# A hybrid retention, gating and gated-MLP layer on one core: every product walks its moving operand as two interleaved halves

## The chip, the cores and the metric

The kernel runs on one core of one Trainium2 chip. The metric is device time in microseconds. The kernel before takes 818.51 us, the median of 3 runs that lie between 818.5 and 818.79 us.

## The reference

One layer over 512 positions of width 1024. All weights and activations are float32.

```python
h = _rmsnorm(x, g_pre_mix)
proj = h @ w_in                       # 1024 x 7168, then split
q, k, v, g, u, sv, a_ret, a_sgu = jnp.split(proj, list(np.cumsum(IN_SPLITS)[:-1]), axis=-1)
y_ret = _retention_branch(q, k, v, g, ret_decay_logit, w_ret_o)
y_sgu = _sgu_branch(u, sv, sgu_ln_g, sgu_ln_b, w_spatial, b_spatial, w_sgu_o)
merged = jax.nn.sigmoid(a_ret) * y_ret + jax.nn.sigmoid(a_sgu) * y_sgu
x = x + _rmsnorm(merged @ w_out, g_post_mix)
h2 = _rmsnorm(x, g_pre_ffn)
x = x + _rmsnorm(_conv_gated_mlp(h2, w_up, conv_w, conv_b, w_down), g_post_ffn)
```

The retention branch has 4 heads, works in chunks of 128 positions and runs over the sequence in both directions. The gating branch mixes positions inside chunks of 128. The MLP has 2816 hidden channels in each of its two halves, with a depthwise convolution over three positions between the up projection and the gate.

## The kernel before

Nearly all of the time goes to products on TensorE. A product, in this text, is one matmul instruction: a stationary operand of 128 x 128, a moving operand of 128 partitions by 512 or 256 columns, and a result in one PSUM bank of 128 partitions by 512 float32. To compute in float32 at TensorE's fast rate for that type, each operand is split into a high and a low part of type float32r: ScalarE writes the high part, VectorE the difference (`split`, L100). A float32 product is then three instructions, high by high, high by low and low by high, that add up in the same bank (`mm3`, L230, and the same triple written out at L340, L543 to L545, L761, L924 to L926, L1169 and L1185).

The stages follow each other in this order:

- 17 warm-up products on constants in bfloat16 (L324).
- The projection to q and k (L342 for the first eighth of the contraction, then `mm3`), 512 columns wide but for the first 24 products, which are 256 wide.
- Six groups of 96 products for v, sv and g (`t_group`, L533), with the retention heads between them (`scores`, `states`, `values`; all 256 wide through `mm3`).
- The projections to u and to the two merge gates, and four fifths of the up projection, in a scheme that computes a 2 x 2 block product with seven smaller products in place of eight (class `Pair`, L746, products at L762, all 256 wide). Between them stand plain blocks of 24 products, 512 wide (`f_block`, L735).
- The output projection (class `Down`, L906, 512 wide), and the second norm.
- The rest of the up projection in `f_block`, and the down projection in the scheme of seven again (`products`, L1156, and `add_whole`, L1176, all 256 wide).

Two kinds of product are not split. Products of whole float32 (L438 and L840, 128 columns) take two instructions each in the profile. Transposes (L522, L668, L685, L992) go through TensorE too.

Weights arrive over one DMA queue in blocks of 128 x 1024 float32 (L149), a few blocks ahead of their use, and are split or summed on ScalarE, VectorE and GpSimd into slots of a rotating buffer. The start addresses of the slots are offset by 64 or 192 bytes for some forms (`AT_64`, `AT_192`, L140; pads at L65). The results in the banks are read by ScalarE and VectorE with plain access patterns over the columns. TensorE's instructions run in the order of the program, which a scheduler keeps to.

The first operand after the output in `nc.tensor.matmul` is the stationary one, the second the moving one. Before the change every moving operand and every output is a plain run of 128, 256 or 512 consecutive columns per partition.

Of the kernel before, what the change touches and what calls it, by code (L numbers as in the profile page):

```python
# [19 lines left out]
KD = D // P  # L20
# [27 lines left out]
def tile_block(ctx: ExitStack, tc, xT, x, wall, par, cs, wsp, bsp, gpost, gffn, out):  # L48
    nc = tc.nc
# [43 lines left out]

    def copy(o, i):
        return nc.scalar.activation(out=o, in_=i, func=AF.Copy)  # L95

    def as32(t):
        return t.bitcast(F32)
# [11 lines left out]
    i = 0  # L110
    while i < NW:
# [7 lines left out]
        elif i == UP0 + 2 * COUPLES[0][0]:  # L119
# [3 lines left out]
            i = UP0 + 2 * COUPLES[-1][1] + 2  # L123
# [104 lines left out]
        return w_ready.pop(i)  # L228

    def mm3(o, ah, al, bh, bl, start, stop, skip=False):  # L230
        nc.tensor.matmul(o, ah, bh, start=start, stop=False, skip_group_check=skip)  # L231
        nc.tensor.matmul(o, ah, bl, start=False, stop=False, skip_group_check=skip)  # L232
        nc.tensor.matmul(o, al, bh, start=False, stop=stop, skip_group_check=skip)  # L233


    part = const("part", [P, NPAR])
# [24 lines left out]
    xh, xl, xg = [], [], {}  # L261
# [15 lines left out]
    def x_low(k, t, f=slice(0, S)):  # L277
        return nc.vector.scalar_tensor_tensor(
            out=xl[k][:, f], in0=t[:, f], scalar=col(PRE + k), in1=as32(xh[k][:, f]), op0=ALU.mult, op1=ALU.subtract
        )  # L280
# [45 lines left out]
    for k in range(KD):  # L326
        if k != 1:
            xts.append(load_x(k))
        if k == 0:
            xts.append(load_x(1))  # L330
        xt = xts[k]
        if k > 1:
            x_low(k, xt)
        if k == 2:
            copy(hold[:, 0:16], as32(xl[1])[:, 0:16])
        wh, wl = w_get(1 if k < 4 else LOOK)
        if k == 0:
            for half in range(2):
                for f in (T0, T1) if half == 0 else (slice(0, S),):
                    for a, b in ((wh, xh), (wl, xh), (wh, xl)):  # L340
                        for m in range(4 * half, 4 * half + 4):
                            nc.tensor.matmul(  # L342
                                qk[m][:, f], a[:, m * P : (m + 1) * P], b[0][:, f],
                                start=a is wh and b is xh and f.start == 0, stop=False, skip_group_check=True,
                            )
            continue
        if k > 1 and (k - 2) % 4 < 2:
            x_scaled(k - 2, xts[k - 2])
        for m in range(8):
            c = slice(m * P, (m + 1) * P)  # L350
            mm3(qk[m], wh[:, c], wl[:, c], xh[k], xl[k], False, k == KD - 1, True)
# [75 lines left out]
    for m in range(8):  # L427
        t = blk(n="qkraw")
# [6 lines left out]

    rb = ps()
    for t in range(NT):
        nc.tensor.matmul(  # L438
            rb[:, t * P : (t + 1) * P],
            rstd[:, t : t + 1].to_broadcast([P, P]),  # L440
            ident,
            start=True,
            stop=True,
        )
# [86 lines left out]
    part_end = [None]  # L531

    def t_group():  # L533

        acc = [ps() for _ in range(NT)]
        for kp in range(4):
            wh, wl = w_get()
            for t in range(NT):
                c = slice(t * P, (t + 1) * P)
                for kk in range(2):  # L540
                    k = 2 * kp + kk
                    f = slice(kk * S, (kk + 1) * S)
                    nc.tensor.matmul(acc[t], xh[k][:, c], wh[:, f], start=k == 0, stop=False)  # L543
                    nc.tensor.matmul(acc[t], xh[k][:, c], wl[:, f], start=False, stop=False)  # L544
                    part_end[0] = nc.tensor.matmul(acc[t], xl[k][:, c], wh[:, f], start=False, stop=k == KD - 1)  # L545
            yield acc

    vh, vl = {}, {}
# [143 lines left out]
    def row_sums():  # L692

        rw = ps()
        for n, w in enumerate(wst_parts):
            i = nc.tensor.matmul(rw, ones, w, start=n == 0, stop=n == 1)
        copy(rws, rw)
        return i.ins


    for h in range(H):
# [3 lines left out]
        acc = next(gen)  # L705
# [8 lines left out]
    ones, one = blk(F32R, "ones", (P, P)), blk(n="one", shape=(P, P))  # L714
# [6 lines left out]
    for n, acc in enumerate(t_group()):  # L721
# [3 lines left out]
        if n < 2:  # L725
            for k in (n + 2, n + 6):
                t = tmp("xT")
# [18 lines left out]
    class Pair:  # L746
# [8 lines left out]
        def product(self, b, act, first, w=None):  # L755
            wh, wl = w or w_get()
            o = self.b[b][:, T0]
            for k in range(4):
                c = slice(k * P, (k + 1) * P)
                h_, l_ = act(k)  # L760
                for n, (w_, a_) in enumerate(((wh, h_), (wh, l_), (wl, h_))):  # L761
                    self.last = nc.tensor.matmul(  # L762
                        o, w_[:, c], a_, start=first and k == n == 0, stop=k == 3 and n == 2,
                        skip_group_check=True,
                    )
            return o
# [53 lines left out]
    for j in range(KD // 2):  # L820
        p = Pair(AF.Gelu_apprx_tanh, lambda: U_HOMES.pop()(), None, rbc)
# [9 lines left out]
    def mix(j):  # L831
        gs = slice((j // 2) * P, (j // 2 + 1) * P)
        add = tmp("add", (P, P))
        v.scalar_tensor_tensor(
            out=add, in0=rws[:, gs], scalar=col(LNB + j), in1=bst[:, gs],
            op0=ALU.mult, op1=ALU.add,
        )
        o = ps()
        for t in range(NT):
            nc.tensor.matmul(  # L840
                o[:, t * P : (t + 1) * P],
                svz[t, j // 4][:, (j % 4) * P : (j % 4 + 1) * P],
                wst[:, gs],
                start=True,
                stop=True,
            )
        m = tmp("mix")
        v.scalar_tensor_tensor(
            out=m.rearrange("p (t q) -> p t q", t=NT),
            in0=o.rearrange("p (t q) -> p t q", t=NT),  # L850
            scalar=col(LNG + j),
            in1=add[:, None, :].to_broadcast([P, NT, P]),
            op0=ALU.mult,
            op1=ALU.add,
        )
        v.tensor_mul(uT[j], m, uT[j])
        h_, l_ = blk(F32R, "yh"), blk(F32R, "yl")
        split(h_, l_, uT[j])
        yh.append(h_)
        yl.append(l_)  # L860
# [22 lines left out]
    for j in range(KD // 2):  # L883
        for o, t in gated_pair(ogh, ogl, late if j == 0 else None):
            b = (lo64("r", F32) if j == 0 else hi192("r", F32) if j < 3 else blk(n="r"))
# [20 lines left out]
    class Down:  # L906
# [13 lines left out]
        def mms(self, t, k, n, bh, bl):  # L920
            c = slice(t * P, (t + 1) * P)
            ah, al = self.a[0][k][:, c], self.a[1][k][:, c]
            o = self.acc[t][n]
            nc.tensor.matmul(o, ah, bh, start=k == 0, stop=False)  # L924
            nc.tensor.matmul(o, ah, bl, start=False, stop=False)
            nc.tensor.matmul(o, al, bh, start=False, stop=k == self.nk - 1)  # L926

        def finish(self, t, n):
            for i, (wh, wl) in enumerate(self.held):
# [100 lines left out]
    for t in range(NT):  # L1030
        acc = [dn_.finish(t, 0)]
# [97 lines left out]
    i = 0  # L1129
    while i < NF:  # L1130
        if i in couples:
            p = Pair(None, lambda: tmp("c"), (h2h, h2l, h2forms))
            p.part1()
            o = [f_block(h2h, h2l, KD)]
# [5 lines left out]
        else:  # L1140
            o = []
# [14 lines left out]
    def products(m, j, steps={}, look=LOOK, ahead=None):  # L1156

        for n, (unit, at, act) in enumerate(UNITS):
            if n in (0, 3):
                with tc.issue_after(ahead) if ahead else ExitStack():  # L1160
                    wh, wl = w_get(look)
            if j == 0:
                m[n] = ps()
            f = slice(at * 256, (at + 1) * 256)
            ah, al = dforms[j][act]
            for t in range(2):
                c = slice(t * P, (t + 1) * P)
                o = m[n][:, t * 256 : (t + 1) * 256]
                for i, (a_, w_) in enumerate(((ah, wh), (ah, wl), (al, wh))):  # L1169
                    nc.tensor.matmul(  # L1170
                        o, a_[:, c], w_[:, f], start=j == t == i == 0,
                        stop=j == DP - 1 and i == 2 and n not in (M2, M3, M4), skip_group_check=True,
                    )
            steps.get(n, lambda: None)()

    def add_whole(m, t, gs, ws, last=False):  # L1176

        c = slice(t * P, (t + 1) * P)
        for n, b in enumerate(((M2, M3), (M4, M8))[t // 2]):
            o = m[b][:, (t % 2) * 256 : (t % 2 + 1) * 256]  # L1180
            for g, (wh, wl) in zip(gs, ws):
                for k in range(2):
                    f = slice(k * S + n * 256, k * S + (n + 1) * 256)
                    ah, al = whole[2 * g + k]
                    for i, (a_, w_) in enumerate(((ah, wh), (ah, wl), (al, wh))):  # L1185
                        nc.tensor.matmul(  # L1186
                            o, a_[:, c], w_[:, f], start=b == M8 and t == 2 and g == k == i == 0,
                            stop=last and g == gs[-1] and k == 1 and i == 2, skip_group_check=True,
                        )
# [27 lines left out]
    for j in range(DP):  # L1217
# [5 lines left out]
        if j in (3, 5):  # L1223
            w = w_get()
# [240 lines left out]
```

## Time and profile before

| | |
|---|---|
| median of 3 runs | 818.51 us |
| span of the profiled execution | 817.4 us |
| its TensorE clock, mean granted | 0.997 |
| TensorE products | 5163 instructions, 809.1 us busy |
| TensorE weight loads | 5163, 730.4 us busy |
| VectorE | 1115, 659.9 us busy |
| ScalarE | 777, 441.3 us busy |
| GpSimd | 93, 86.0 us busy |
| DMA | 93.24 MB, 114 GB/s on average |

The profile is one execution of the program. Times in its rows count from the start of the span. PE is TensorE's products, PEld its weight loads, DVE is VectorE, ACT is ScalarE, POOL is GpSimd. A row names the line of the kernel, the operation, the output and the inputs by the program's names, the size, and a count. Products overlap: the duration of one is longer than the distance to the next, so the rate of a stream of products is read from the distance between two starts.

### The profile page before, as it was taken

How to read it: one execution, taken by the hardware profiler on the slowest of the kernel's cores; microseconds unless marked ns; L12 is line 12 of the kernel's file. 1: busy time of each engine (PE TensorE's matmuls, PEld its weight loads, DVE VectorE, ACT ScalarE, POOL GpSimd, SP SyncE). 2: the span in 40 equal slices, each digit the busy share in tenths (PEclk: the TensorE clock that was granted, in tenths of full speed). 3: DMA queues.
4: the chain of work that ended last, by engine and by line, in shares of the span. 5: the costliest groups of instructions: out<-in, count | busy, mean ns of one | idle time of the engine just before them, and what ended most of it. 6: DMA issues, size and time to landing. Idle time of an engine off the chain costs nothing. (4 is left out here: it accounts for less than half of the span.)

```text
span 817.4 us, 13292 instructions
## 1 busy us (share of the span) xinstructions
PE 809.1 (99%) x5163; PEld 730.4 (89%) x5163; DVE 659.9 (81%) x1115; ACT 441.3 (54%) x777; POOL 86.0 (11%) x93
## 2 busy tenths in 40 slices
PE   9999999999999999999999999999999999999996
PEld 7888888888999999999988898899999898999996
DVE  7479897877898777767765659989999989987877
ACT  6546445536675444444445577556666666544441
POOL 0010000110001111132210210110111200000001
PEclk9999999999999999999999999999999999999998
DMA  8733222221333332233349111333333341233244
GB/s 287 259 117 103 78 79 77 77 79 65 103 103 105 104 103 90 91 103 103 107 165 335 53 51 66 104 103 104 104 103 103 103 156 52 77 130 110 97 155 155
DMA packets 29647, 93.24 MB, mean 114 GB/s; under 512 B 3536, under 2 KB 4432, under 8 KB 29584
## 3 DMA queue, kind: packets, MB, share of 16 engines
q1 hardware_dynamic: 27360, 86.76, 31.5%
q0 software_dynamic: 1360, 4.46, 1.6%
q10 hardware_dynamic: 864, 1.18, 0.4%
q8 instruction: 40, 0.66, 0.3%
q14 instruction: 23, 0.19, 0.1%
HBM read 88.19 MB, written 4.19 MB: 113 GB/s over the span
## 5 line engine op out<-in xcount | busy, mean ns | idle before, releaser
L102 DVE TENSOR_TENSOR wl<-raw,wh 128x1024 fp32r<-128x1024 f32 (+1 forms) x92 | 108.5, 1187 | 42.5 <-PE ps L762 20.0
L95 ACT ACTIVATE wf<-raw 128x512 fp32r<-128x512 f32 x140 | 85.0, 626 | 99.3 <-PE ps L232 34.0
L102 DVE TENSOR_TENSOR wf<-raw,wf 128x512 fp32r<-128x512 f32 x140 | 106.5, 773 | 25.3 <-ACT wf L95 24.5
L762 PE MATMUL ps<-sh,wf 128*128 128x256 f32 x640 | 118.8, 277 | 0.2 <-ACT c L95 0.2
L95 ACT ACTIVATE wh<-raw 128x1024 fp32r<-128x1024 f32 (+2 forms) x96 | 93.3, 983 | 39.2 <-PE ps L545 15.8
L762 PEld LDWEIGHTS ps<-sh,wf 128*128 128x128 f32 x640 | 100.9, 188 | 1.0 <-ACT c L95 0.4
L232 PE MATMUL ps<-h2l,wh 128*128 128x512 f32 (+1 forms) x256 | 92.5, 363 | 0.0
L231 PE MATMUL ps<-h2h,wh 128*128 128x512 f32 (+1 forms) x256 | 92.4, 364 | 0.0
L233 PE MATMUL ps<-h2h,wl 128*128 128x512 f32 (+1 forms) x256 | 92.3, 361 | 0.0
L762 PE MATMUL ps<-sl,wf 128*128 128x256 f32 x320 | 88.5, 277 | 0.0
L543 PE MATMUL ps<-wh,xh 128*128 128x512 f32 x192 | 75.0, 391 | 0.0
L544 PE MATMUL ps<-wl,xh 128*128 128x512 f32 x192 | 74.8, 390 | 0.0
L545 PE MATMUL ps<-wh,xl 128*128 128x512 f32 x192 | 74.7, 389 | 0.0
L762 PEld LDWEIGHTS ps<-sl,wf 128*128 128x128 f32 x320 | 60.1, 188 | 0.6
L1170 PE MATMUL ps<-dl,fh 128*128 128x256 f32 x216 | 59.8, 277 | 0.0
L1170 PE MATMUL ps<-dh,fh 128*128 128x256 f32 x216 | 59.7, 277 | 0.0
L1170 PE MATMUL ps<-dh,fl 128*128 128x256 f32 x216 | 59.7, 277 | 0.0
L233 PEld LDWEIGHTS ps<-h2h,wl 128*128 128x128 f32 x256 | 48.0, 188 | 7.7
L231 PEld LDWEIGHTS ps<-h2h,wh 128*128 128x128 f32 x256 | 47.8, 188 | 7.2 <-ACT h2h L994 0.3
L232 PEld LDWEIGHTS ps<-h2l,wh 128*128 128x128 f32 x256 | 48.1, 188 | 6.6
L762 PE MATMUL ps<-xh,wf 128*128 128x256 f32 x288 | 53.9, 278 | 0.0
L95 ACT ACTIVATE dh<-raw 128x768 fp32r<-128x768 f32 (+1 forms) x36 | 33.6, 949 | 34.4 <-DVE raw L204 18.9
(314 smaller groups left out, 2037.4 us busy)
## 6 DMA issues: line engine op xcount, KB each, us to landing
raw<-wall SPq DMA_DIRECT2D x144, 512.0 KB, 3.6
x<-x SPq DMA_DIRECT2D x24, 256.0 KB, 6.2
x<-x POOLq DMA_DIRECT2D x8, 256.0 KB, 2.4
xT<-xT SPq DMA_DIRECT2D x7, 256.0 KB, 4.7
xT<-xT POOLq DMA_DIRECT2D x4, 256.0 KB, 3.3
out<-zg SPq DMA_DIRECT2D x4, 256.0 KB, 2.0
raw<-wall SPq DMA_DIRECT2D x3, 256.0 KB, 4.7
out<-zs ACTq DMA_DIRECT2D x3, 256.0 KB, 2.4
```

The lines of the kernel that those rows point to most:

```text
L95: return nc.scalar.activation(out=o, in_=i, func=AF.Copy)
L102: nc.vector.tensor_sub(lo, src, as32(hi))
L231: nc.tensor.matmul(o, ah, bh, start=start, stop=False, skip_group_check=skip)
L232: nc.tensor.matmul(o, ah, bl, start=False, stop=False, skip_group_check=skip)
L233: nc.tensor.matmul(o, al, bh, start=False, stop=stop, skip_group_check=skip)
L543: nc.tensor.matmul(acc[t], xh[k][:, c], wh[:, f], start=k == 0, stop=False)
L544: nc.tensor.matmul(acc[t], xh[k][:, c], wl[:, f], start=False, stop=False)
L545: part_end[0] = nc.tensor.matmul(acc[t], xl[k][:, c], wh[:, f], start=False, stop=k == KD - 1)
L762: self.last = nc.tensor.matmul(o, w_[:, c], a_, start=first and k == n == 0, stop=k == 3 and n == 2, skip_group_check=True,)
L1170: nc.tensor.matmul(o, a_[:, c], w_[:, f], start=j == t == i == 0, stop=j == DP - 1 and i == 2 and n not in (M2, M3, M4), skip_group_check= ...
```

## The change

Two helpers are new. `two` regards the columns of an operand as two halves (n), each cut into pairs (c, with e the place in the pair), and orders them by pair first and half second: columns 0 and 1, then the first two of the second half, then columns 2 and 3, and so on. `mm` is a matmul whose output and moving operand are both regarded so. The stationary operand is not touched. As both are walked in the same order, each result lands in the column where it landed before, and the readers of the banks are unchanged.

```diff
     def copy(o, i):
         return nc.scalar.activation(out=o, in_=i, func=AF.Copy)
+
+    def two(t):
+        return t.rearrange("p (n c e) -> p c n e", n=2, e=2)
+
+    def mm(o, a, b, **kw):
+        return nc.tensor.matmul(two(o), a, two(b), **kw)
...
     def mm3(o, ah, al, bh, bl, start, stop, skip=False):
-        nc.tensor.matmul(o, ah, bh, start=start, stop=False, skip_group_check=skip)
-        nc.tensor.matmul(o, ah, bl, start=False, stop=False, skip_group_check=skip)
-        nc.tensor.matmul(o, al, bh, start=False, stop=stop, skip_group_check=skip)
+        mm(o, ah, bh, start=start, stop=False, skip_group_check=skip)
+        mm(o, ah, bl, start=False, stop=False, skip_group_check=skip)
+        mm(o, al, bh, start=False, stop=stop, skip_group_check=skip)
...
-                    nc.tensor.matmul(acc[t], xh[k][:, c], wh[:, f], start=k == 0, stop=False)
-                    nc.tensor.matmul(acc[t], xh[k][:, c], wl[:, f], start=False, stop=False)
-                    part_end[0] = nc.tensor.matmul(acc[t], xl[k][:, c], wh[:, f], start=False, stop=k == KD - 1)
+                    mm(acc[t], xh[k][:, c], wh[:, f], start=k == 0, stop=False)
+                    mm(acc[t], xh[k][:, c], wl[:, f], start=False, stop=False)
+                    part_end[0] = mm(acc[t], xl[k][:, c], wh[:, f], start=False, stop=k == KD - 1)
...
                 for n, (w_, a_) in enumerate(((wh, h_), (wh, l_), (wl, h_))):
-                    self.last = nc.tensor.matmul(
+                    self.last = mm(
                         o, w_[:, c], a_, start=first and k == n == 0, stop=k == 3 and n == 2,
                         skip_group_check=True,
                     )
```

In the same way `nc.tensor.matmul` becomes `mm` in the first eighth of the q and k projection (L342), at L438, L696 and L840, in `Down.mms` (L924 to L926), in `products` (L1170) and in `add_whole` (L1186). The warm-up products and the transposes stay as they were. Half of a 512-wide operand lies 1024 bytes behind the other half, half of a 256-wide one 512 bytes.

More of the change, by code (lines that the diff above doesn't have):

```diff
@@ L341, in tile_block @@
                         for m in range(4 * half, 4 * half + 4):
-                            nc.tensor.matmul(
+                            mm(
                                 qk[m][:, f], a[:, m * P : (m + 1) * P], b[0][:, f],
@@ L437, in tile_block @@
     for t in range(NT):
-        nc.tensor.matmul(
+        mm(
             rb[:, t * P : (t + 1) * P],
@@ L695, in row_sums @@
         for n, w in enumerate(wst_parts):
-            i = nc.tensor.matmul(rw, ones, w, start=n == 0, stop=n == 1)
+            i = mm(rw, ones, w, start=n == 0, stop=n == 1)
         copy(rws, rw)
@@ L839, in mix @@
         for t in range(NT):
-            nc.tensor.matmul(
+            mm(
                 o[:, t * P : (t + 1) * P],
@@ L923, in mms @@
             o = self.acc[t][n]
-            nc.tensor.matmul(o, ah, bh, start=k == 0, stop=False)
-            nc.tensor.matmul(o, ah, bl, start=False, stop=False)
-            nc.tensor.matmul(o, al, bh, start=False, stop=k == self.nk - 1)
+            mm(o, ah, bh, start=k == 0, stop=False)
+            mm(o, ah, bl, start=False, stop=False)
+            mm(o, al, bh, start=False, stop=k == self.nk - 1)
         def finish(self, t, n):
@@ L1169, in products @@
                 for i, (a_, w_) in enumerate(((ah, wh), (ah, wl), (al, wh))):
-                    nc.tensor.matmul(
+                    mm(
                         o, a_[:, c], w_[:, f], start=j == t == i == 0,
@@ L1185, in add_whole @@
                     for i, (a_, w_) in enumerate(((ah, wh), (ah, wl), (al, wh))):
-                        nc.tensor.matmul(
+                        mm(
                             o, a_[:, c], w_[:, f], start=b == M8 and t == 2 and g == k == i == 0,
```

## The prediction

> **What bounds the kernel now.** I read the page's totals first, then the waits of TensorE, then single products in order of time, then the busy time by stretches.
>
> ```profile
> span 817.4 us, 13292 instructions
> PE 809.1 (99%) x5163; PEld 730.4 (89%) x5163; DVE 659.9 (81%) x1115; ACT 441.3 (54%) x777; POOL 86.0 (11%) x93
> PE ps L762 <- ACT c L95: 0.2, 1, 0.2
> 741.88 55.99 PE ps L1170 x492
> ...
> 797.88 2.73 PE ps L1186 x24
> 800.63 0.43 DVE z L1267
> ```
>
> The first two lines are the page's head: TensorE is busy for 809.1 of 817.4 us. The third is from the list of TensorE's waits: once its first product has run, one wait of 0.2 us is all there is. The others are from the chain that ended last: products stand back to back until 800.63 us, then comes a tail of some 17 us of VectorE and GpSimd work. The span is therefore a warm-up, a stream of products without a hole, and a tail. A share of busy time says nothing about how fast the stream itself flows, so I look at the distance from start to start.
>
> ```profile
> 40.58 0.39 PE L231 MATMUL ps<-xh,wh 128*128 128x512 f32 x1
> ...
> 43.98 0.39 PE L231 MATMUL ps<-xh,wh 128*128 128x512 f32 x1
> 742.40 0.28 PE L1170 MATMUL ps<-dh,fh 128*128 128x256 f32 x1
> ...
> 743.99 0.28 PE L1170 MATMUL ps<-dh,fl 128*128 128x256 f32 x1
> ```
>
> These are rows of the timeline: start, duration, line, operands. Between the first two lie 15 steps, 3.40 / 15 = 226.7 ns for 512 columns. Between the last two lie 14 steps, 1.59 / 14 = 113.6 ns for 256 columns; twice that is 227.2. So the time is proportional to the columns, 0.443 ns each, and a product has no fixed part that the trace can show. A start at a new address, which every product makes, costs at most (227.2 - 226.7) = 0.5 ns.
>
> Is it the array or its supply that sets 0.443 ns? The first microseconds tell.
>
> ```profile
> 0.76 3.79 PE L324 MATMUL ps<-const-bfloat16-1.0 128*128 128x256 bf16 x17 [0.76 <-PEq L1455]
> 5.88 0.96 PE L342 MATMUL ps<-xh,wl 128*128 128x256 f32 x4
> 6.68 0.64 PE L342 MATMUL ps<-xl,wh 128*128 128x256 f32 x4
> 7.16 0.64 PE L342 MATMUL ps<-xh,wh 128*128 128x256 f32 x4
> 7.63 0.64 PE L342 MATMUL ps<-xh,wl 128*128 128x256 f32 x4
> L324 PE MATMUL ps<-const-bfloat16-1.0 x17: 372/421/421, 0.8 to 4.1; 128*128 128x256 bf16 x17
> ```
>
> The 17 warm-up products of 256 bf16 columns start (3.79 - 0.42) / 16 = 211 ns apart. Four f32 products that begin at 5.88 us take 0.80 us to the next group, 200 ns each, and those at 6.68 us take 0.48, 120 ns each. I read that as an array at half speed until about 6.4 us (the granted clock is given as 1.00 there too, so this rests on the steps alone). At half speed f32 is as fast as bf16. At full speed half of 211, 106 ns, would be due (an estimate), and f32 gets 113.6. The f32 stream is thus 6 to 7% slower than the array, and only when the array runs fast: the supply of the moving operand is at its limit. A change of the order in which that operand is read touches just this limit.
>
> **The change part by part.** Nothing is added or removed: each product keeps its stationary operand, columns, sums and place in the queue. The DMAs, semaphores and readers of the banks are the same, and column c of a bank still holds column c. What changes is the walk, two columns from the first half of the operand, two from the second, and so on; the bank is written in that order. A 512-wide product makes 256 runs of two in place of one run of 512.
>
> How many columns does it touch? By the loops: 512 wide are 180 in the first projection, 576 in six groups at L543 to L545, 384 for the gate outputs, 192 at L924 to L926, 576 for the up projection and 2 at L696, 1910 in all. The page's 5163 less these, 17 warm-up, 80 transposes and 72 at L438 and L840 leaves 3084 of 256 wide. That is 1910 x 512 + 3084 x 256 = 1,767,000 columns. At 0.443 ns they take 783 us, which with warm-up, tail and small products makes up the span.
>
> The price of a run of two does not show in this trace, as every run there is 128 columns or longer. Bounds:
>
> - Below, a gain: the walk lets the supply keep up. The 512-wide products could come down to the array's estimate, 211 ns at the lowest. The 256-wide ones could not go under what their weight loads allow; the nearest row is the transposes, which load 128 columns for every product:
>
> ```profile
> 72.12 0.60 PE L522 MATMUL ps<-ident,rot 128*128 128x128 f32 x4
> L522 PE MATMUL ps<-ident,rot x16: 270/272/273, 72.1 to 159.8; 128*128 128x128 f32 x16
> ```
>
> (0.60 - 0.27) / 3 = 110 ns. The gain is at most 1910 x (226.7 - 211) + 3084 x (113.6 - 110) = 30 + 11 = 41 us.
>
> - In the middle, nothing: a new address at each product's start is free within 0.5 ns, as shown. But that address is known one product ahead, while here it changes every 0.9 ns.
>
> - Above, a loss: the nearest row for a slow moving operand is the full f32 product at L840.
>
> ```profile
> L840 PE MATMUL ps<-wst,sv 128*128 128x128 f32 x64 | 7.8, 275 | 0.0
> L840 PE MATMUL ps<-wst,sv x64: 270/275/275, 273.3 to 341.9; 128*128 128x128 f32 x64
> ```
>
> 7.8 / 64 = 122 ns for 128 columns, 0.95 ns each, and the cold f32 products above have 200 / 256 = 0.78. If a supply that is just enough for long runs hands over one piece of consecutive words per step and only half of the piece is used, a column costs 2 x 0.443 = 0.886 ns, between these two rows. The columns then take 1566 us, 783 more.
>
> I take the upper value. The reason is the reading above: the supply has no reserve (it is 6% short already), so any piece that is longer than two words would now be fetched twice, and there is no slack into which the second fetch could go. Nothing covers it, as TensorE has no holes. The other engines have more time than before, so no wait moves elsewhere. The sum: 817.4 + 783 = 1600 us for the profiled execution; 1.1 us lie around its span by the median of 818.51, so 1601 us. With the two rows as bounds for a column (0.78 to 0.95) the forecast's own range is 1410 to 1710; I expect it near the factor of two, 1500 to 1610.
>
> One rule speaks against the change on the other side, the bank. The Trainium skill, "PSUM — Partial Sum Buffer", section "Specifications (TRN2)", says that PSUM lines are 8 bytes and that any non-contiguous access pattern slows matmuls significantly. Pairs fill such a line, so by the line's size the write would cost nothing and by the rule's second half it would cost something unknown; no row here has a non-contiguous bank write, and the sum above would stand or grow.
>
> **The rivals.**
>
> *No change.* If the supply's step is two words or less, the order of steps does not matter, the products keep 226.7 and 113.6 ns, and the time stays at 818.5 us. For it: free starts at product boundaries. Against it: a supply that is 6% short on long runs hints at something paid per piece of memory. The Trainium skill, "Vector Engine (DVE) Microarchitecture Reference", section "5.2 Measured stream behaviour on trn2 (trn3 not measured)", states that an engine port streams at full rate when neighbouring 4-byte words come in runs of two or more from an 8-byte boundary, with any hop between free. It was measured for VectorE; if it held here, this rival would be the result.
>
> *Faster.* If the 6% are lost where one stretch of memory is left for the next, two stretches in turn could hide that. The 512-wide products would go to 211 ns and the 256-wide ones to 110, 41 us less. But VectorE would become the bound in the stretch of the up projection:
>
> ```profile
> 500.00:700.00 200.00, 199.83 (x1213) 177.84 (x1212) 188.85 (x299) 123.36 (x209) 22.68 (x15) 1.00 0.30 98
> 700.00:800.00 100.00, 100.00 (x871) 99.65 (x870) 82.16 (x132) 46.28 (x70) 1.13 (x2) 1.00 0.35 116
> ```
>
> VectorE's busy time is the third pair: 188.85 of 200 us. A stream 5% faster would need 190, so VectorE's uneven waits would show; I take off 5 us. That gives 818.5 - 36 = 782 us. For it: the 6% are there to be had. Against it: nothing in the trace shows that short runs help.
>
> *A part slower.* The walk could lose something smaller per product, as the products at 7.16 us do, which read at another place than the later ones: 480 / 4 = 120 ns against 113.6. Over 1,767,000 / 256 = 6900 units this is 6900 x 6.4 ns = 44 us, 863 us; the case decides as soon as a unit of 256 columns loses 0.3 ns (2 us in all). At its far end, half of the pieces fetched twice, it is 1.5 x 783, 1210 us.
>
> *The fast f32 mode is lost.* Were the broken walk run like the full f32 products at L840, two passes of 0.95 ns each, the columns would take 1,767,000 x 1.9 ns = 3360 us. I know no reason; it is the form in which the change would not do what it says.
>
> **How the numbers follow.** Forecast (a column costs about double) 0.43, a part slower 0.13, fast mode lost 0.01, no change 0.13, faster 0.30. A measurement of this kernel can tell 0.2%, 1.6 us, from no change. So slower 0.57, same 0.13, faster 0.30. The range has to take in cases of both signs: from 780 (the faster rival at its full size) to 1640 (the forecast and a little more per pair). It leaves out the lost mode and a column cost near 0.95 ns, under 0.1 together; a low end at the no-change time would leave out a further 0.30, too much.
>
> **What would show it.** Right: in the timeline the 512-wide products start about 453 ns apart and the 256-wide ones about 227, in all stages alike, while transposes keep 110 and the stretch before 6 us is nearly as before (at half speed the supply has reserve); VectorE's, ScalarE's and GpSimd's busy times stay and their shares halve; TensorE still has no waits. If the 256-wide and 512-wide products differ per column, the price lies in the collision of moving reads and weight loads and not in the runs. Wrong: a step of 226.7 ns unchanged means a supply that does not care about order, and one near 213 that the 6% belonged to long runs.

## The result, and the profile after

The changed kernel takes 1178.94 us (median of 4 runs, 1177.92 to 1179.15), the one before 818.50 us. The ratio is 1.4401, with a 95% interval from 1.4381 to 1.4421. It is slower, as forecast, but by 360 us and not by 783.

First the head of the page of the changed kernel, and the list of TensorE's waits in it (engine, line, what was waited for: total us, times, longest).

```profile
span 1177.3 us, 13314 instructions
PE 1169.2 (99%) x5163; PEld 904.6 (77%) x5163; DVE 664.2 (56%) x1115; ACT 445.2 (38%) x777; POOL 82.0 (7%) x93
PE ps L330 <- PEq L1461: 0.8, 1, 0.8
```

TensorE runs the same 5163 products, is busy for 99% of a longer span, and waits for nothing once it has started. The other engines do the same work in the same time (VectorE 664.2 us against 659.9), with smaller shares. So the whole difference is in how fast products follow each other. The timeline shows it (start, duration, line, operands); every changed product now has the line of the helper, L101.

```profile
59.81 0.50 PE L101 MATMUL ps<-xh,wl 128*128 128x512 f32 x1
...
64.81 0.50 PE L101 MATMUL ps<-xh,wl 128*128 128x512 f32 x1
1059.77 0.33 PE L101 MATMUL ps<-dh,fh 128*128 128x256 f32 x1
...
1062.40 0.33 PE L101 MATMUL ps<-dl,fh 128*128 128x256 f32 x1
```

Between the first two rows lie 15 steps: 5.00 / 15 = 333.3 ns for 512 columns, where it was 226.7. Between the last two lie 16: 2.63 / 16 = 164.4 ns for 256 columns, where it was 113.6. That accounts for the change: 1910 x 106.6 + 3084 x 50.8 = 204 + 157 = 361 us, and the span grew by 1177.3 - 817.4 = 359.9. A column costs 0.65 and 0.64 ns. The transposes, which the change leaves alone, and the first products, which the prediction reads as an array at half speed, are in the same timeline:

```profile
5.54 1.04 PE L101 MATMUL ps<-xh,wl 128*128 128x256 f32 x4
6.40 0.87 PE L101 MATMUL ps<-xl,wh 128*128 128x256 f32 x4
7.10 0.85 PE L101 MATMUL ps<-xh,wh 128*128 128x256 f32 x4
7.78 0.85 PE L101 MATMUL ps<-xh,wl 128*128 128x256 f32 x4
101.56 0.61 PE L528 MATMUL ps<-ident,rot 128*128 128x128 f32 x4
```

From 5.54 to 6.40 us four products take 0.86 us, 215 ns each. The 200 ns that the prediction has for this stretch before the change average in a product of the faster pace. These are the starts of the kernel before, four steps apart (x2: a row that takes in the next product too):

```profile
5.45 0.64 PE L342 MATMUL ps<-xh,wh 128*128 128x256 f32 x2
...
6.31 0.54 PE L342 MATMUL ps<-xh,wl 128*128 128x256 f32 x2
```

0.86 / 4 = 215 ns here too: in the slow stretch the new walk costs nothing. From 7.10 to 7.78 us the products take 170 ns each, where it was 120. That the stretch ends with the clock, as the prediction reads it, has a sign in the trace: its record of the granted clock begins only at 6.61 us before the change and at 6.45 us after it, and the steps shorten there. The transposes keep (0.61 - 0.275) / 3 = 112 ns.

### The profile page after: what moved, and what is told of

Its sections match the earlier page's. It is cut to its first block, busy times and chain, and to the rows that moved or that the text cites. A ratio compares the mean times of both kernels' runs of the same rounds, so it can differ in the third digit from the quotient of the medians.

```text
span 1177.3 us, 13314 instructions
## 1 busy us (share of the span) xinstructions
PE 1169.2 (99%) x5163; PEld 904.6 (77%) x5163; DVE 664.2 (56%) x1115; ACT 445.2 (38%) x777; POOL 82.0 (7%) x93
## 4 chain that ended last, share of the span: by engine, by line
PE 99%; issue 0%; DVE 0%; POOLq 0%; POOL 0%; DVEq 0%
PE ps L101 98%; PE ps L330 0%; PE ps L998 0%; PE ps L528 0%; PE ps L691 0%; PE ps L674 0%; DVE zs L1323 0%; POOLq L1467 0%; DVE zg L1323 0%; POOL qr L1291 0%; DVE z L1273 0%; DVEq L1467 0%; DVE qs L1290 0%
## 5 line engine op out<-in xcount | busy, mean ns | idle before, releaser
L101 PE MATMUL ps<-sh,wf 128*128 128x256 f32 x640 | 169.1, 337 | 0.0
L101 PEld LDWEIGHTS ps<-sh,wf 128*128 128x128 f32 x640 | 117.2, 195 | 2.2
L101 PE MATMUL ps<-h2l,wh 128*128 128x512 f32 (+1 forms) x256 | 118.3, 463 | 0.0
L101 PE MATMUL ps<-h2h,wl 128*128 128x512 f32 (+1 forms) x256 | 118.3, 463 | 0.0
L101 PE MATMUL ps<-h2h,wh 128*128 128x512 f32 (+1 forms) x256 | 118.1, 463 | 0.0
L101 PE MATMUL ps<-sl,wf 128*128 128x256 f32 x320 | 107.4, 336 | 0.0
L101 PE MATMUL ps<-wh,xh 128*128 128x512 f32 x192 | 96.9, 505 | 0.0
L101 PE MATMUL ps<-wl,xh 128*128 128x512 f32 x192 | 96.8, 504 | 0.0
L101 PE MATMUL ps<-wh,xl 128*128 128x512 f32 x192 | 96.8, 504 | 0.0
L101 PE MATMUL ps<-xh,wf 128*128 128x256 f32 x288 | 76.6, 340 | 0.0
L101 PE MATMUL ps<-dh,fl 128*128 128x256 f32 x216 | 72.1, 334 | 0.0
L101 PE MATMUL ps<-dh,fh 128*128 128x256 f32 x216 | 71.8, 333 | 0.0
L101 PE MATMUL ps<-dl,fh 128*128 128x256 f32 x216 | 71.8, 333 | 0.0
L101 PEld LDWEIGHTS ps<-h2h,wl 128*128 128x128 f32 x256 | 50.0, 196 | 26.5
L108 DVE TENSOR_TENSOR dl<-raw,dh 128x768 fp32r<-128x768 f32 (+1 forms) x36 | 39.2, 1090 | 51.6 <-PE ps L101 50.4
L101 PEld LDWEIGHTS ps<-h2h,wh 128*128 128x128 f32 x256 | 49.9, 195 | 23.5 <-ACT h2h L1000 0.3
L101 PEld LDWEIGHTS ps<-h2l,wh 128*128 128x128 f32 x256 | 50.0, 196 | 23.2
L101 PEld LDWEIGHTS ps<-sl,wf 128*128 128x128 f32 x320 | 62.4, 195 | 2.2
```

What stands on the lines that cost most here:

```text
L101: return nc.tensor.matmul(two(o), a, two(b), **kw)
L108: nc.vector.tensor_sub(lo, src, as32(hi))
```

## The experiments

All edits are made to the changed kernel's two helpers. In each run the kernel before was timed on the same chip, with medians from 818.49 to 818.89 us. "Step" is the distance between starts of 512-wide products near 60 us (40 us for the kernel before), taken from the rows shown; for the eights and the thirty-twos the 15 steps run from 59.77 to 63.42 and from 59.83 to 63.38 us. It differs by some 2% from stage to stage.

| run | moving operand's walk | bank's walk | us | step, ns |
|---|---|---|---|---|
| before | plain | plain | 818.5 | 226.7 |
| changed kernel | pairs, 2 halves in turn | the same | 1178.94 | 333.3 |
| read only | pairs, 2 halves in turn | plain | 1177.78 | 328.7 |
| write only | plain | pairs, 2 halves in turn | 818.58 | 226.7 |
| fours | fours, 2 halves in turn | the same | 900.75 | 250.0 |
| skip read | even pairs, then odd pairs | plain | 1598.74 | 450.9 |
| no return | even pairs of 2 halves in turn, then odd pairs (512-wide only) | the same | 1351.1 | 2 x 251 |
| quarters | pairs, 4 quarters in turn | the same | 1569.55 | 443.6 |
| eights | eights, 2 halves in turn | the same | 874.72 | 243.3 |
| sixteens | sixteens, 2 halves in turn | the same | 859.93 | 240.0 |
| twice | first pair of each four, twice | plain | 818.63 | 226.7 |
| skip fours | even fours, then odd fours | plain | 840.39 | 231.3 |
| only 256 | changed on 256-wide products | the same | 984.08 | not changed |
| thirty-twos | 32 elements, 2 halves in turn | the same | 850.23 | 236.7 |

**Reading or writing?** The two sides of the walk were taken apart.

```diff
-        return nc.tensor.matmul(two(o), a, two(b), **kw)
+        return nc.tensor.matmul(o, a, two(b), **kw)
```

> Only the moving operand is walked as interleaved halves; the bank is written in a plain run, so each bank's columns come out permuted. The changed kernel spends 333.3 ns per 512 columns, 0.416 ns more per pair than before (226.7). Theory A (the supply of the moving read pays for each short run): about 1179 us, 512-wide products 333 ns apart. Theory B (the bank write pays for each short run): about 818 us, 227 ns. Theory C (the instruction's walk pays, whichever side has it): about 1179 us here and in the write-only run.

```diff
-        return nc.tensor.matmul(two(o), a, two(b), **kw)
+        return nc.tensor.matmul(two(o), a, b, **kw)
```

> Only the bank is written as interleaved halves; the moving operand is read in a plain run, so each bank's columns come out permuted. A: about 818 us, 512-wide products 227 ns apart. B: about 1179 us, 333 ns. C: about 1179 us.

Two rows of the timeline of each, the first and the last of 15 steps; the read-only run first.

```profile
59.69 0.51 PE L101 MATMUL ps<-xh,wl 128*128 128x512 f32 x1
...
64.62 0.51 PE L101 MATMUL ps<-xh,wl 128*128 128x512 f32 x1
```

```profile
59.66 0.39 PE L101 MATMUL ps<-wh,xl 128*128 128x512 f32 x1
...
63.06 0.39 PE L101 MATMUL ps<-wh,xl 128*128 128x512 f32 x1
```

4.93 / 15 = 328.7 ns against 3.40 / 15 = 226.7. The ratios to the kernel before are 1.4393 (1.4364 to 1.4422) and 1.0003 (0.9993 to 1.0014). The 4.6 ns between this step and the changed kernel's 333.3 belong to the stage: from 149.78 to 152.78 us the read-only run has nine steps of 333.3 ns, and the two times differ by 0.1%. The read carries the whole price and the write in pairs from two halves none. Theories B and C fall.

**Is a piece fetched twice?** The forecast rested on a supply that hands over more than two words at a time. In the skip read the pairs of one place are taken 16 bytes apart, so a piece of four words would be fetched for each pair, with no second place.

```diff
     def two(t):
-        return t.rearrange("p (n c e) -> p c n e", n=2, e=2)
+        return t.rearrange("p (c n e) -> p n c e", n=2, e=2)
...
-        return nc.tensor.matmul(two(o), a, two(b), **kw)
+        return nc.tensor.matmul(o, a, two(b), **kw)
```

> Only the moving operand's walk is changed, and there are no two distant places: pairs 0, 2, 4 and so on of the whole operand, then pairs 1, 3, 5; the bank is written in a plain run, so its columns come out permuted. If A is right and a run of two costs because a piece of four words is fetched for it: as in the read-only run. If A is right but it is the jump between two halves that costs: about 818 us. If B is right: 818 us.

```profile
59.49 0.63 PE L101 MATMUL ps<-xl,wh 128*128 128x512 f32 x1
...
64.45 0.63 PE L101 MATMUL ps<-xh,wh 128*128 128x512 f32 x1
```

These rows are 11 steps apart: 4.96 / 11 = 450.9 ns, twice a plain run. The outcome is neither of the two that A allowed: the price is not that of the read-only run, and it is not nothing. It is a full doubling, 1598.74 us, ratio 1.9537 (1.9498 to 1.9577). A place of its own makes it worse, so two halves in turn help somewhere. The counterpart reads one pair of each four twice in a row:

```diff
-        return t.rearrange("p (n c e) -> p c n e", n=2, e=2)
+        q = t.rearrange("p (c q) -> p c q", q=4)
+        return q[:, :, None, 0:2].to_broadcast([P, q.shape[1], 2, 2])
...
-        return nc.tensor.matmul(two(o), a, two(b), **kw)
+        return nc.tensor.matmul(o.rearrange("p (c n e) -> p c n e", n=2, e=2), a, two(b), **kw)
```

> The moving operand is read as the first pair of each four columns, twice; the second pair of each four is left out, so half of the columns are missing in every product. The address goes back after every two columns, 256 times per 512 columns as in the skip read, but only 128 pieces of four words are touched, each twice in a row. D (time goes with the fetches of pieces; a second visit finds its piece): as a plain run, 227 ns per 512 columns, about 818 us. If it is the run of two itself that costs, whatever it reads: 453 ns, about 1600 us, or 333 ns and 1179 us.

```profile
59.83 0.39 PE L102 MATMUL ps<-wh,xh 128*128 128x512 f32 x1
...
63.23 0.39 PE L102 MATMUL ps<-wh,xh 128*128 128x512 f32 x1
```

3.40 / 15 = 226.7 ns, ratio 0.9997 (0.9987 to 1.0007). The address jumps after every second column, 256 times per product as in the skip read, and it costs nothing. So what is paid for is the number of pieces fetched, 128 here and in a plain run, 256 in the skip read, and not the jump. The next run fixes the size of a piece.

```diff
-        return t.rearrange("p (n c e) -> p c n e", n=2, e=2)
+        return t.rearrange("p (c n e) -> p n c e", n=2, e=4)
...
-        return nc.tensor.matmul(two(o), a, two(b), **kw)
+        return nc.tensor.matmul(o, a, two(b), **kw)
```

> Only the read is changed: pieces of four words 0, 2, 4 and so on, then 1, 3, 5, so each is fetched once, in one place, but no two neighbours follow each other; the bank's columns come out permuted. Fours from two halves cost 250 ns per 512 columns. If the 23 ns there come from turning between two places: 227 ns, 818 us. If any piece that isn't the next one costs them: 250 ns, 901 us.

```profile
59.82 0.39 PE L101 MATMUL ps<-wh,xh 128*128 128x512 f32 x1
...
63.29 0.39 PE L101 MATMUL ps<-wh,xh 128*128 128x512 f32 x1
```

3.47 / 15 = 231.3 ns, and 840.39 us, between the two expectations and nearer to the lower. With a piece of eight words this walk would have doubled the time; it adds 2.6% (ratio 1.0262, 1.0241 to 1.0283). So a piece holds four words, 16 bytes. A fetch takes 450.9 / 256 = 1.76 ns in the skip read, and a plain run leaves 226.7 / 128 = 1.77 ns for each, next to no reserve.

**Why 333 and not 453?** Two theories were left: a piece just fetched is kept for its second visit (D), or reads from two places overlap (E).

```diff
+    def mm(o, a, b, start, stop, **kw):
+        if b.shape[-1] < S:
+            return nc.tensor.matmul(o, a, b, start=start, stop=stop, **kw)
+        def turn(t, m):
+            return t.rearrange("p (n c m e) -> p m c n e", n=2, m=2, e=2)[:, m]
+        nc.tensor.matmul(turn(o, 0), a, turn(b, 0), start=start, stop=False, **kw)
+        return nc.tensor.matmul(turn(o, 1), a, turn(b, 1), start=False, stop=stop, **kw)
```

> Only the 512-wide products are changed; the 256-wide ones read in a plain run. Each 512-wide product is split into two of 256 columns with the same stationary operand: the first reads the even pairs, from the first and the second half in turn, the second the odd pairs. So places alternate as in the changed kernel, but no piece of four words is visited again soon. Theory D (a piece of four words costs 1.77 ns to fetch, as in the skip read, 453 ns for 256 pieces; a piece just fetched is kept, and its second visit costs only the array's 0.83 ns; 128 x 1.77 + 128 x 0.83 = 333): every visit is a fetch, 2 x 227 ns, so 1910 x (453 - 227) = 432 us more than before, 1250 us. Theory E (reads from two places overlap, and any pair costs 1.30 ns when places alternate): 2 x 167 ns, 1910 x (333 - 227) = 203 us more, 1021 us.

```profile
59.79 0.44 PE L102 MATMUL ps<-xh,wh 128*128 128x256 f32 x1
60.05 0.43 PE L103 MATMUL ps<-xh,wh 128*128 128x256 f32 x1
...
63.56 0.44 PE L103 MATMUL ps<-xl,wh 128*128 128x256 f32 x1
```

From the first to the last row are 15 steps: 3.77 / 15 = 251 ns for 256 columns, so 502 ns for what was one product. With 1351.1 us it is slower than D's 1250 and far from E's 1021. E falls: without the quick second visit, two places in turn are no faster than one (450.9 ns), but slower.

```diff
-        return t.rearrange("p (n c e) -> p c n e", n=2, e=2)
+        return t.rearrange("p (n c e) -> p c n e", n=4, e=2)
```

> Both walks take pairs from four quarters in turn instead of two halves, so a piece is visited again after three others. D with two kept pieces: no second visit finds its piece any more, 453 ns per 512 columns as in the skip read, about 1600 us. D with four or more: as in the changed kernel, about 1179 us. E: 1179 us, or less if more places overlap better.

```profile
59.65 0.62 PE L101 MATMUL ps<-xl,wh 128*128 128x512 f32 x1
...
64.53 0.62 PE L101 MATMUL ps<-xh,wh 128*128 128x512 f32 x1
```

4.88 / 11 = 443.6 ns, close to the 453 of D with few kept pieces. So when three other pieces come between its visits, a piece is paid for again, at 443.6 / 256 = 1.73 ns a visit. When one comes between, the second visits cost (333.3 - 226.7) / 128 = 0.83 ns on average, less than half of a fetch. The distance between the places does not make the difference: the quarters of a 512-wide operand lie 512 bytes apart, as do the halves of a 256-wide one, which has the low price of 0.64 ns per column in the changed kernel. That a piece is kept is the account that fits; a trace does not show the keeping itself. Whether two or three pieces are kept was not tried. The no-return run and the quarters change the bank's walk too, and their walks of the bank were not timed alone; only pairs from two halves were.

**What does turning between places cost by itself?** Runs of four and more fetch each piece once, so what remains is the turning.

```diff
-        return t.rearrange("p (n c e) -> p c n e", n=2, e=2)
+        return t.rearrange("p (n c e) -> p c n e", n=2, e=4)
```

> Both walks as in the changed kernel, but four neighbouring elements at a time. If a short run is paid for by the run (one array cycle, 0.416 ns, each): half as many runs, 512-wide products 226.7 + 128 x 0.416 = 280 ns apart, 818 + 180 = 998 us. If what is paid for is a piece of four words of which a run of two uses half: nothing is lost any more, 227 ns, about 818 us.

The next three differ from it in one number, e=8, e=16 and e=32.

> Both walks as in the changed kernel with eight neighbouring elements at a time. Fours cost 901 us, 23 ns per 512 columns over a plain run, 0.18 ns for each of 128 runs. If each jump between places costs that: 64 runs, 11.5 ns, 818 + 41 = 860 us. If the loss is that of a piece's alignment with pairs of pieces, it is gone: 818 us.

> The same with sixteen elements, 64 bytes. If each jump costs 0.18 ns: 32 runs, 5.8 ns per 512 columns, 838 us. If jumps are free at this length: 818 us. If the 6% by which a plain run is slower than the array is lost at borders of memory that two places in turn would hide: under 818 us, at best about 780.

> Both walks as in the changed kernel, 32 elements (128 bytes) at a time. Sixteens cost 13.3 ns per 512 columns over a plain run, 0.42 ns for each of 32 runs. If a run costs that: 16 runs, 6.7 ns, 818 + 23 = 841 us. If longer runs have no more to give: 860 us as with sixteens. Under 818 us would speak for a loss at borders that two places hide.

The first and last of 15 steps of the fours, and then of the sixteens:

```profile
59.75 0.42 PE L101 MATMUL ps<-wh,xl 128*128 128x512 f32 x1
...
63.50 0.41 PE L101 MATMUL ps<-wh,xl 128*128 128x512 f32 x1
```

```profile
59.83 0.40 PE L101 MATMUL ps<-wh,xl 128*128 128x512 f32 x1
...
63.43 0.40 PE L101 MATMUL ps<-wh,xl 128*128 128x512 f32 x1
```

The steps are 250.0 and 240.0 ns. All four are slower than a plain run, with ratios 1.1008 (1.0989 to 1.1026), 1.0683 (1.0667 to 1.0699), 1.0502 (1.0484 to 1.0519) and 1.0382 (1.0367 to 1.0398). No expectation was met to the microsecond: fours lie between the two that were written, and eights (875 for 860), sixteens (860 for 838) and thirty-twos (850 for 841) cost more than a fixed price per run. Eight times fewer runs, from fours to thirty-twos, cut the loss only from 82 to 31 us. The price of one turn between two halves thus grows with the run's length, for a reason that stays open. Four quarters in turn show no such price: 1.73 ns a visit, against 250 / 128 = 1.95 in the fours and 1.76 in the skip read. So turning as such is not what costs, and what it is about two halves stays open too.

**Do the two kinds of product add up?**

```diff
+        if b.shape[-1] != 256:
+            return nc.tensor.matmul(o, a, b, **kw)
         return nc.tensor.matmul(two(o), a, two(b), **kw)
```

> The change on the 256-wide products alone. They were 113.6 ns apart before and are about 164.9 with the change: 3084 x 51.3 ns = 158 us, 976 us in all, if the two kinds add up (the 512-wide: 1910 x 106.6 = 204 us; 158 + 204 = 362, measured 360). If something else than the products takes part, the sum won't hold.

```profile
869.83 0.34 PE L103 MATMUL ps<-wh,fl 128*128 128x256 f32 x1
...
872.85 0.34 PE L103 MATMUL ps<-wh,fl 128*128 128x256 f32 x1
```

984.08 us, ratio 1.2017 (1.1997 to 1.2037): 165 us more than before, for 158 expected. The rows, 18 steps apart in the down projection, give 3.02 / 18 = 167.8 ns, where the changed kernel has 164.4: 3084 x (167.8 - 113.6) = 167 us. Why the same walk takes 3 ns more in this run stays open. With the 204 us that the step gives for the 512-wide ones, which were not run alone, the sum is 369, 9 more than the change cost. So the loss is that of the products themselves, within 3%.

## Why the prediction was wrong in size

- **The stream is the bound, and nothing covers a loss in it.** Right. TensorE has no waits after its start, and the steps of the two kinds of product alone give 361 of 360 us.
- **The supply of the moving operand, not the array, sets the step.** Right for the changed kernel: the read alone carries the price, in the slow stretch the new walk costs nothing (215 ns before and after), and at full pace 170 against 120.
- **"The f32 stream is thus 6 to 7% slower than the array."** Not borne out. The 106 ns for 256 columns were an estimate, half of a slow step. In the quarters and the thirty-twos the record of the granted clock begins at 3.79 and 3.90 us, before the last two warm-up products start, so that one bf16 step of each is at full pace. In the quarters:

```profile
3.86 0.39 PE L330 MATMUL ps<-const-bfloat16-1.0 128*128 128x256 bf16 x2
3.97 0.27 PE L330 MATMUL ps<-const-bfloat16-1.0 128*128 128x256 bf16 x1
```

The starts in the trace are 114 ns apart, and 113 in the thirty-twos: bf16 is no faster than f32 with its 113.6. These are the only two bf16 steps at full pace, and what bounds them is not shown. But nothing here shows that a plain run is short of supply. What it lacks is reserve, and that the skip read shows (1.76 ns a fetch, where a plain run has 1.77). The price that the forecast gave to a second fetch thus came out right on a ground that it did not have, which is luck.

- **The supply hands over pieces longer than two words.** Right: four words. The forecast price for a piece fetched twice, 0.886 ns per column and 1601 us, is what the skip read measures, 1598.74.
- **"Any piece that is longer than two words would now be fetched twice."** This step failed. With two halves in turn, only one other piece comes between the two visits of a piece, and the second visit then costs less than half of a fetch. A column costs 0.65 ns in place of 0.886, and the change 360 us in place of 783. How the 333 ns divide was not measured, and several sums fit: 128 fetches at 1.77 and 128 second visits at 0.83; 128 visits that fetch at 1.95, as in the fours, and second visits at 0.65; or half of the second visits fetched again at the quarters' 1.73, 192 x 1.73 = 332.
- **The far end of the rival "a part slower"** was worked out as half of the pieces fetched twice, 1210 us. That number came closest, and second visits at half the price on average are near what was measured; whether it is half of the pieces that are fetched twice, the sums above leave open. The rival gave no reason for the half, so its number is partly luck. It was given 0.13, beside a forecast that allowed the supply no memory at all.
- **No change.** Fell, and with it the transfer of the rule in the Trainium skill, "Vector Engine (DVE) Microarchitecture Reference", section "5.2 Measured stream behaviour on trn2 (trn3 not measured)", that runs of two or more neighbouring 4-byte words from an 8-byte boundary stream at full rate with any hop between. It was measured for VectorE; for TensorE's moving operand such runs are not free here: 1.44 for two halves, 1.95 for pairs 16 bytes apart. What is free is a hop that goes back to the same piece (ratio 0.9997).
- **Faster.** Fell for this form of walk: every walk with two places in turn, from 2 to 32 elements, is slower than a plain run. The 6% that were to be had rest on the estimate above, which the two bf16 steps do not bear out.
- **The bank.** The rule in the Trainium skill, "PSUM — Partial Sum Buffer", section "Specifications (TRN2)", that any non-contiguous pattern slows matmuls, is not borne out for pairs from two halves: 1.0003 for the write-only run. The 8 bytes that it gives for a line are in keeping with that; no run here writes the bank in single words.
- **The other engines** nearly kept their busy times, as expected. Their shares fell by a third and not by half, with the span.

## What to carry to other kernels

When a stream of products has no holes, compare its step with the array's own and ask which side feeds it. Here a split float32 moving operand is read in pieces of 16 bytes at some 1.76 ns each, which leaves no reserve at full pace, so each fetched piece should be used whole and in order. The bank can be written in pairs from two halves at no cost, so a permutation of that kind belongs there and not on the moving side. And an estimate of the array's own pace should be checked on a step of the trace before a rival of the size of the gap is given weight.

## What was not expected of the hardware

- Pairs 16 bytes apart from one place cost 451 ns per 512 columns, pairs from two halves in turn 333 and from four quarters 444: on the account that a fetched piece is kept, at least one is held behind the current one, and fewer than would serve four places.
- Pieces used whole cost 227 ns per product in a plain run, 231 with every second piece skipped, and 250 when two halves take turns, so it is mostly the two places that cost, not the skipping. Yet four quarters in turn, in pairs, cost no more per visit than one place.
- Runs of 16 and 32 elements from two halves still lose 13 and 10 ns per 512 columns, though they turn four and eight times less often than fours, which lose 23.
